# Attention weights times values in two float32r passes, with the values kept as high and low halves side by side

## Chip, core and metric

The program runs on one core of a Trainium2 chip. The metric is the device time of one execution in microseconds; lower is better. Engines are named as in the profile: PE (TensorE), PEld (its weight loads), DVE (VectorE), ACT (ScalarE), POOL (GpSimd), SP (the queue that issues the transfers).

## What is computed

The reference is two blocks of two layers each on 512 tokens of width 1024. The first block has an RWKV layer and a layer of banded attention, each followed by a convolutional feed-forward layer. The second has a layer with two kinds of attention (differential and sparse) and a layer of latent attention. Two places matter here: the banded attention (16 heads of 64, 4 key/value heads, a window of 128) and the sparse one (8 heads of 64 over one shared value head).

```python
def swa_sink_attention(x, k, v, w_q, sinks, w_o):
    ...
    s = jnp.einsum('bnqhgd,bnkhd->bnhgqk', q, kb) * (HEAD_DIM ** -0.5)
    s = jnp.where(mask, s, NEG_INF)
    m = jnp.maximum(jnp.max(s, axis=-1, keepdims=True), sk)
    p = jnp.exp(s - m)
    denom = jnp.sum(p, axis=-1, keepdims=True) + jnp.exp(sk - m)
    o = jnp.einsum('bnhgqk,bnkhd->bnqhgd', p / denom, vb)
    return o.reshape(B, T, ATTN_HEADS * HEAD_DIM) @ w_o

def dsa_attention(...):        # per block of 128 queries, over the selected keys
    ...
    p = jax.nn.softmax(s, axis=-1)
    return jnp.einsum('bhqk,bqkd->bqhd', p, v_sel)
```

## The kernel before

Everything lies feature-major: 1024 features as 8 tiles of 128 partitions by 512 tokens. A dense product keeps its operands as a high and a low part in float32r and runs three passes (`mm3`, L375 to L377); `split` (L322) makes the two parts, the high one with an ACT copy (L325), the low one with a DVE subtraction (L326). Weights arrive by SP, are split the same way (`wload`), and `ahead` loads the next ones early.

**Banded attention** (`swa`, L1365). The work is eight items (`gp`, `blk`): two pairs of key/value heads by four blocks of 128 queries. `scores(it)` makes for each of 8 heads two PE passes (L1407, L1408), a DVE reduction that adds the mask and takes the row's minimum (`submin`, L1502), an ACT exponential (L1410) and a scaling, on POOL for even heads (L1396) and on DVE for odd ones (L1398, after a reciprocal, L1394). `values(it)` turns the probabilities with PE transposes (L1427), copies each 128x512 tile from PSUM with ACT (L1429), multiplies it with 64 columns of the values in plain float32 (L1435: two heads write the two halves of one PSUM tile `po`) and splits `po` into the operand of the output projection (L325, L326). Items are woven: the loop at L1481 runs the values of item i-1 beside the scores of item i (`even` spreads their steps), beside the two late query tiles (`late`) for the first three rounds, and beside the first half of the output projection's first two tiles (`begun`) for the last four. Eight PSUM tiles are shared by all (`ps`, L310). `V` is filled with one ACT copy for each token tile (L1476).

**Sparse attention** (`dsa_parts`, L1744). Four blocks of queries, 3 down to 0. `scores` is as above (L1783, L1784, L1502, L1789), with a bias that POOL adds to the selection (L1776). `values(qb)` turns the probabilities (`turn`, L1807), copies them with ACT (L1811) or, for the last blocks, DVE (L1809), multiplies with `vb` in float32 (L1826), multiplies with gate and denominator `g` on DVE (L1829) and splits (L1830). Values of a block run beside the scores of the next. The projection `w_eo` follows, and its first tiles begin on heads that are done.

The order of the instructions on each engine is fixed when the program is built, by the weaving above and a scheduler that knows the dependences; an engine waits at the head of its queue.

Of the kernel before, what the change touches and what calls it, by code (L numbers as in the profile page):

```python
# [9 lines left out]
F32 = mybir.dt.float32  # L10
F32R = mybir.dt.float32r
AF = mybir.ActivationFunctionType
ALU = mybir.AluOpType
# [4 lines left out]
T = 512  # L18
# [3 lines left out]
TT = 4  # L22
# [216 lines left out]
def run(gen):  # L239
    for _ in gen:  # L240
        pass
# [42 lines left out]
HALF = slice(0, 64), slice(64, 128)  # L284


class Net:
# [1077 lines left out]
    def swa(self):  # L1365
        nc = self.nc
        ident = self.ident
        with self.pool("sw_a") as ap, ExitStack() as es:
            qT = ap.tile([128, 2, KT, T], F32R, name="qT")
            kT = ap.tile([128, 2, 2, T], F32R, name="kT")  # L1370
            kL = ap.tile([128, 2, 2, T], F32R, name="kL")
            V = ap.tile([128, TT, 256], F32, name="V")
            msk = ap.tile([128, 256], F32, name="msk")
            nc.sync.dma_start(out=msk, in_=self.i["c_swa"])
            self.bias_rows()
# [41 lines left out]
            def values(it):  # L1417
                gp, blk = it
                k0 = 0 if blk else 1
                S = SS.pop(it)  # L1420
                PT = {}
                for e in range(2):
                    for kc in range(k0, 2):
                        pt = self.ps()
                        for hg in range(4):
                            o = (kc - k0) * 128
                            nc.tensor.transpose(pt[:, hg * 128 : hg * 128 + 128], S[:, e, hg, o : o + 128], ident)  # L1427
                        PT[e, kc] = op.tile([128, 512], F32, tag="PT", name=self.nm("PT"), bufs=6)
                        nc.scalar.activation(PT[e, kc], pt, AF.Copy)  # L1429
                        yield  # L1430
                po = self.ps()
                for kc in range(k0, 2):
                    for e in range(2):
                        g = 2 * gp + e
                        nc.tensor.matmul(po[64 * e : 64 * e + 64], V[:, blk - 1 + kc, g * 64 : g * 64 + 64], PT[e, kc], start=kc == k0, stop=kc == 1)  # L1435
                    yield
                q = slice(blk * 128, blk * 128 + 128)
                oh, ol = out[gp]
                self.split(oh[:, :, q], ol[:, :, q], po[:].rearrange("p (h q) -> p h q", h=4))
                yield  # L1440

            def query(m, ps, pool):
# [18 lines left out]
            items = [(gp, blk) for gp in range(2) for blk in range(TT)]  # L1461
            with self.pool("sw_p") as pp:
                pss, rr, row = self.first
                row = self.row_sb(row)
                xk = self.hilo(pp, KT, "xk")
                for j in range(KT):
                    self.split(xk[j][0], xk[j][1], self.x[:, j], scale=self.vec("kv_g", j))
                for m in range(2):
                    ps = self.dense_fm(self.i["w_kk"][m], xk, then=self.i["w_kk"][1] if m == 0 else self.i["w_kv"][0][:, :1024])
                    t = pp.tile([128, T], F32, tag="t", name=self.nm("t"), bufs=2)  # L1470
                    nc.vector.tensor_tensor(out=t, in0=ps, in1=row, op=ALU.mult)
                    self.twice(kT[:, :, m], kL[:, :, m], t)
                    for i in range(3 * m, 3 * m + 3):
                        query(i, pss[i], pp)
                even((self.dense_tm(self.i["w_kv"][0], xk, 256,
                                    lambda tt, ps: nc.scalar.activation(V[:, tt], ps[:, :256], AF.Copy, scale=rr[:, tt : tt + 1])), 8), (scores(items[0]), 9))  # L1476
            op = es.enter_context(self.pool("sw_o"))
            out = {0: [op.tile([128, 4, T], F32R, name=f"o{q}0") for q in "hl"]}
            q67 = late()
            begun = chain(*(self.begin(self.i["w_oa"], [(out[0][0][:, j], out[0][1][:, j]) for j in range(4)], m, 4) for m in range(2)))  # L1480
            for i in range(1, 9):  # L1481
                live = [(values(items[i - 1]), 7)]
                if i < 8:
                    live.append((scores(items[i]), 9))
                if i < 4:
                    live.append((take(q67, 6), 6))
                if i == 4:
                    run(q67)
                    out[1] = qT[:, 0, :4], qT[:, 1, :4]
                if i > 4:  # L1490
                    live.append((take(begun, 2), 2))
                even(*live)
# [3 lines left out]
            flat = [qT[:, e, 4:].rearrange("p m t -> p (m t)") for e in range(2)] + [kT[:].rearrange("p e m t -> p (e m t)")]  # L1496
            yg = [t for _ in range(2) for t in self.by_tile(sp.tile([128, 4, T], F32, tag="S", name=self.nm("yg"), bufs=2))]
            self.project(self.i["w_oa"], xs, "ng11", yg, "ng12", 4, "ffn1", [[t[:, f * 1024 : f * 1024 + 1024] for f in range(2)] for t in flat])

    def submin(self, out, ps, mask, mn, first=3e38):  # L1500

# [242 lines left out]
    def dsa_parts(self, ap, qb_, kb, vb, sel, gate):  # L1744

        nc = self.nc
        ident = self.ident
        bts, SS, WD = {}, {}, {}

        head = lambda i: 2 * (i % 4) + i // 4  # L1750

        def load(i):
            bts[head(i)] = self.bias_tile(4 + head(i), ap, f"bias{i}")
# [43 lines left out]
        def values(qb):  # L1797
            q = slice(qb * 128, qb * 128 + 128)
            S, wide = SS.pop(qb), WD.pop(qb)
            PT = {}  # L1800

            def turn(kc):
                PT[kc] = self.wp.tile([128, 2, T], F32, tag="wl", name=self.nm("PT"))
                for e in range(2):
                    pt = self.ps()
                    for j in range(4):
                        nc.tensor.transpose(pt[:, j * 128 : j * 128 + 128], S[:, 4 * e + j, kc * 128 : kc * 128 + 128], ident)  # L1807
                    if qb == 0 or qb < 2 and e:
                        nc.vector.tensor_copy(PT[kc][:, e], pt)  # L1809
                    else:  # L1810
                        nc.scalar.activation(PT[kc][:, e], pt, AF.Copy)  # L1811
                    yield

            yield from turn(0)

            row = self.ps()
            for j in range(4):
                nc.tensor.transpose(row[:, j * 128 : j * 128 + 128], wide[:, j].rearrange("p e d -> p (e d)"), ident)
            g = self.sp.tile([128, 4, 128], F32, tag="sssq", name=self.nm("g"), bufs=2)
            nc.vector.tensor_tensor(out=g, in0=row[:].rearrange("p (h q) -> p h q", h=4), in1=gate[:, 4:, q], op=ALU.mult)  # L1820
            po = self.ps()
            for kc in range(qb + 1):
                if kc < qb:
                    yield from turn(kc + 1)
                for e in range(2):
                    nc.tensor.matmul(po[64 * e : 64 * e + 64], vb[:, kc, 8:72], PT[kc][:, e], start=kc == 0, stop=kc == qb)  # L1826
                yield
            y = self.sp.tile([128, 4, 128], F32, tag="ssacc", name=self.nm("y"), bufs=2)
            nc.vector.tensor_tensor(out=y, in0=po[:].rearrange("p (h q) -> p h q", h=4), in1=g, op=ALU.mult)  # L1829
            self.split(self.oh[:, 4:, q], self.ol[1][:, :, q], y[:])  # L1830
            yield

        return prep(), [((scores(n, qb), 9), (values(qb), 3 * qb + 4), None) for n, qb in enumerate((3, 2, 1, 0))]
# [221 lines left out]
```

## Time and profile before

| | |
|---|---|
| median of 3 runs | 1983.86 us (1981.19 to 1985.35) |
| profiled execution | 1977.79 us, span 1976.0 us |
| granted PE clock, mean | 0.985 |
| PE busy | 1883.4 us, 95% of the span |
| DVE busy | 1337.9 us, 68% |
| ACT busy | 956.5 us, 48% |
| POOL busy | 335.9 us, 17% |
| chain that ended last | PE 76%, DVE 15%, issue 3%, ACT 3%, DMA 2% |
| banded attention, items woven | 899.9 to 971.6 us of the span |
| sparse attention, values | 1619.4 to 1656.8 us |

A busy share is an average over stages with different limits, so the two stretches in the last rows are read by themselves: busy time by engine there, then which engine's instructions follow each other without a hole, then at what spacing they start. Instructions of one engine overlap a little: the start of one to the start of the next is shorter than the time that a row gives for one.

### The profile page before, as it was taken

To read this page: it belongs to the slowest core of one execution; us is meant where nothing else is said; L and a number is where in the kernel's file an instruction comes from. 1 tells how busy PE (TensorE), PEld (TensorE's weight loads), DVE (VectorE), ACT (ScalarE), POOL (GpSimd) and SP (SyncE) were. 2 spreads that over 40 slices of the span, in tenths; PEclk is the share of its full clock that TensorE was granted. 3 is DMA by queue.
4 is the path that set the end of the run, shared out by engine and by line. 5 is a ranking of instruction groups with operands and counts; after the bars stand their busy time and mean duration, and the time that the engine had idled before them with its cause. 6 is when DMAs were issued, how large, how long until landed. Compare 5 with 4: busy or idle time off the path is not lost.

```text
span 1976.0 us, 28014 instructions
## 1 busy us (share of the span) xinstructions
PE 1883.4 (95%) x10610; PEld 1491.1 (75%) x10610; DVE 1337.9 (68%) x2618; ACT 956.5 (48%) x1818; POOL 335.9 (17%) x385
## 2 busy tenths in 40 slices
PE   6999878999999999989999999999999999999998
PEld 4784457788888888966688888889788657787657
DVE  7759888767977742677577777525799566356765
ACT  4546344565644432557655444324443475346662
POOL 3347330432000000133120000000304022010000
PEclk9999988999999999999999999999999989999999
DMA  3230101053332333421123332334422113221102
GB/s 115 91 123 26 44 1 32 20 176 99 107 95 97 97 95 98 133 89 54 42 74 100 106 96 96 90 99 129 156 83 86 48 49 116 89 96 57 40 23 86
DMA packets 55424, 165.53 MB, mean 84 GB/s; under 512 B 6182, under 2 KB 11942, under 8 KB 55290
## 3 DMA queue, kind: packets, MB, share of 16 engines
q1 hardware_dynamic: 55290, 163.76, 26.7%
q8 instruction: 83, 1.36, 0.3%
q14 instruction: 51, 0.42, 0.1%
HBM read 161.61 MB, written 2.13 MB: 83 GB/s over the span
## 4 chain that ended last, share of the span: by engine, by line
PE 76%; DVE 15%; issue 3%; ACT 3%; DMA 2%; POOL 1%; DVEq 0%; POOLq 0%; SPq 0%; ACTq 0%
PE ps L375 19%; PE ps L377 18%; PE ps L376 18%; PE ps L448 5%; DVE wl L326 2%; PE ps L1953 2%; PE ps L1984 1%; DVE x L595 1%; PE ps L1435 1%; PE ps L1971 1%; PE ps L1689 1%; ACT wh L325 1%; DVE xl L329 1%; DVE AB L1159 1%; DVE yg L594 1%
## 5 line engine op out<-in xcount | busy, mean ns | idle before, releaser
L326 DVE TENSOR_TENSOR wl<-wr,wh 128x1024 fp32r<-128x1024 f32 (+2 forms) x279 | 328.0, 1176 | 249.9 <-ACT wh L325 243.1
L325 ACT ACTIVATE wh<-wr 128x1024 fp32r<-128x1024 f32 (+2 forms) x279 | 278.8, 999 | 425.8 <-PE ps L376 288.8
L375 PE MATMUL ps<-xh,wh 128*128 128x512 f32 x856 | 338.8, 396 | 0.0
L377 PE MATMUL ps<-xh,wl 128*128 128x512 f32 x856 | 335.7, 392 | 0.0
L376 PE MATMUL ps<-xl,wh 128*128 128x512 f32 x856 | 332.6, 389 | 0.0
L377 PEld LDWEIGHTS ps<-xh,wl 128*128 128x128 f32 x856 | 160.7, 188 | 37.3
L376 PEld LDWEIGHTS ps<-xl,wh 128*128 128x128 f32 x856 | 160.8, 188 | 35.9 <-issue 1.1
L375 PEld LDWEIGHTS ps<-xh,wh 128*128 128x128 f32 x856 | 160.9, 188 | 33.1 <-issue 1.9
L504 POOL TENSOR_TENSOR rr<-rs,mhalf 128x2 f32<-128x2 f32 (+1 forms) x18 | 19.9, 1108 | 891.8 <-DVE rs L502 874.9
L377 PE MATMUL ps<-hidh,wl 128*128 128x512 f32 (+1 forms) x440 | 152.7, 347 | 1.3 <-DVE wl L326 1.3
L375 PE MATMUL ps<-hidh,wh 128*128 128x512 f32 (+1 forms) x440 | 152.8, 347 | 0.0
L376 PE MATMUL ps<-hidl,wh 128*128 128x512 f32 (+1 forms) x440 | 152.5, 347 | 0.0
L1355 DVE SCALAR_TENSOR_TENSOR cv<-h,vecs,cv 128x510 f32<-128x510 f32 (+1 forms) x176 | 130.5, 747 | 2.9 <-ACT cv L1353 0.6
L448 PE MATMUL ps<-xh,wl 128*128 128x512 f32 (+1 forms) x306 | 104.3, 346 | 5.3 <-DVE wl L326 5.3
L448 PE MATMUL ps<-xh,wh 128*128 128x512 f32 (+1 forms) x306 | 103.4, 347 | 3.0 <-ACT xh L328 3.0
L448 PE MATMUL ps<-xl,wh 128*128 128x512 f32 (+1 forms) x306 | 104.2, 343 | 0.0
L1351 DVE TENSOR_TENSOR h<-ps,row 128x512 f32<-128x512 f32 x88 | 60.1, 686 | 60.3 <-PE ps L377 60.3
L377 PEld LDWEIGHTS ps<-hidh,wl 128*128 128x128 f32 x440 | 83.3, 189 | 12.1 <-DVE wl L326 1.7
L375 PEld LDWEIGHTS ps<-hidh,wh 128*128 128x128 f32 x440 | 83.3, 189 | 10.5
L376 PEld LDWEIGHTS ps<-hidl,wh 128*128 128x128 f32 x440 | 83.3, 189 | 10.2
L1353 ACT ACTIVATE cv<-h,vecs 128x512 f32<-128x512 f32 x88 | 71.3, 812 | 11.7 <-DVE h L1351 11.3
L325 ACT ACTIVATE hidh<-cv 128x512 fp32r<-128x512 f32 x44 | 27.7, 630 | 91.9 <-DVE cv L1359 91.8
(467 smaller groups left out, 4152.5 us busy)
## 6 DMA issues: line engine op xcount, KB each, us to landing
wr<-in_w_up SPq DMA_DIRECT2D x76, 512.0 KB, 3.5
wr<-in_w_down SPq DMA_DIRECT2D x40, 448.0 KB, 3.4
wr<-in_w_down SPq DMA_DIRECT2D x20, 512.0 KB, 3.5
wr<-in_w_e SPq DMA_DIRECT2D x20, 512.0 KB, 3.6
wr<-in_w_or SPq DMA_DIRECT2D x16, 512.0 KB, 3.6
wr<-in_w_upg SPq DMA_DIRECT2D x16, 384.0 KB, 3.0
bias<-brow SPq DMA_DIRECT2D x20, 256.0 KB, 4.2
wr<-in_w_oa SPq DMA_DIRECT2D x9, 512.0 KB, 3.6
```

The lines of the kernel that those rows point to most:

```text
L325: nc.scalar.activation(hi, src, AF.Copy)
L326: nc.vector.tensor_tensor(out=lo, in0=src, in1=hi.bitcast(F32), op=ALU.subtract)
L329: nc.vector.scalar_tensor_tensor(out=lo, in0=src, scalar=scale, in1=hi.bitcast(F32), op0=ALU.mult, op1=ALU.subtract)
L375: mm(out, ah, bh, start=start, stop=False)
L376: mm(out, ah, bl, start=False, stop=False)
L377: mm(out, al, bh, start=False, stop=stop)
L448: self.nc.tensor.matmul(pss[m][:, tok], w[a][:, c], xs[j][b][:, tok], start=j == 0 and i == 0 and tok.start == 0, stop=j == KT - 1 and i == 2,
L504: nc.gpsimd.tensor_tensor(out=rr[:, a:b], in0=rs[:, a:b], in1=self.mhalf[:, a:b], op=ALU.pow)
L1351: nc.vector.tensor_tensor(out=h, in0=ps, in1=row, op=ALU.mult)
L1353: nc.scalar.activation(t, h, AF.Identity, bias=self.vec(f"cb{l}", m), scale=self.vec(f"cw{l}2", m))
L1355: nc.vector.scalar_tensor_tensor(out=t[:, d:], in0=h[:, : T - d], scalar=self.vec(f"cw{l}{2 - d}", m), in1=t[:, d:], op0=ALU.mult, op1=ALU ...
L1953: nc.tensor.matmul(ps[:, :w], qh[:, qb * 128 : qb * 128 + 128], kh[:, :w], start=True, stop=True)
```

## The change

In both attentions the transposed probabilities are kept as a high and a low part (`split`: an ACT copy and a DVE subtraction for each 128x512 tile, instead of one copy). The values too are kept as two float32r parts, side by side as 128 columns. `two_pass` multiplies them: one pass with the high, one with the low part of the probabilities, so that the upper half of the PSUM tile holds the product with the values' high part and the lower half that with the low part. Each head group has a PSUM tile of its own, two for an item instead of one. `joined` adds the halves: for each of the two tiles an ACT copy of one half (64x512) and a DVE addition of the other. In the sparse attention the product with `g` moves from DVE to POOL. The values' parts are made by an ACT copy and a DVE subtraction for each token tile (banded) or by one ACT copy and one POOL subtraction (sparse). The steps of `values` are regrouped (a product is issued one step after its splits), and the shares of the weaving go from 7 to 6 or 4 steps.

```diff
-            V = ap.tile([128, TT, 256], F32, name="V")
+            V = ap.tile([128, TT, 4, 2, 64], F32R, name="V")
...
-                PT = {}
-                for e in range(2):
-                    for kc in range(k0, 2):
+                late = []
+                po = [self.ps() for _ in range(2)]
+                for kc in range(k0, 2):
+                    for e in range(2):
                         pt = self.ps()
                         for hg in range(4):
                             o = (kc - k0) * 128
                             nc.tensor.transpose(pt[:, hg * 128 : hg * 128 + 128], S[:, e, hg, o : o + 128], ident)
-                        PT[e, kc] = op.tile([128, 512], F32, tag="PT", name=self.nm("PT"), bufs=6)
-                        nc.scalar.activation(PT[e, kc], pt, AF.Copy)
+                        ph, pl = (op.tile([128, 512], F32R, tag="P" + n, name=self.nm("P" + n), bufs=3) for n in "hl")
+                        self.split(ph, pl, pt)
+                        late.append((po[e], V[:, blk - 1 + kc, 2 * gp + e], ph, pl, kc == k0, kc == 1))
+                        if len(late) > 1:
+                            self.two_pass(*late.pop(0))
                         yield
-                po = self.ps()
-                for kc in range(k0, 2):
-                    for e in range(2):
-                        g = 2 * gp + e
-                        nc.tensor.matmul(po[64 * e : 64 * e + 64], V[:, blk - 1 + kc, g * 64 : g * 64 + 64], PT[e, kc], start=kc == k0, stop=kc == 1)
-                    yield
+                self.two_pass(*late.pop(0))
+                yield
                 q = slice(blk * 128, blk * 128 + 128)
                 oh, ol = out[gp]
-                self.split(oh[:, :, q], ol[:, :, q], po[:].rearrange("p (h q) -> p h q", h=4))
+                y = self.joined(po)
+                self.split(oh[:, :, q], ol[:, :, q], y[:].rearrange("p (h q) -> p h q", h=4))
                 yield
...
+    def two_pass(self, out, v, ph, pl, start, stop):
+        v = v.rearrange("p a b -> p (a b)")
+        self.nc.tensor.matmul(out, v, ph, start=start, stop=False)
+        self.nc.tensor.matmul(out, v, pl, start=False, stop=stop)
+
+    def joined(self, po):
+        nc = self.nc
+        y = self.sp.tile([128, T], F32, tag="ssacc", name=self.nm("yj"), bufs=2)
+        for e in range(2):
+            own, other = HALF[e], HALF[1 - e]
+            nc.scalar.activation(y[own], po[e][other], AF.Copy)
+            nc.vector.tensor_tensor(out=y[own], in0=po[e][own], in1=y[own], op=ALU.add)
+        return y
+
+    def parts_of_values(self, dst, src, scale):
+        nc = self.nc
+        hi, lo = dst[:, :, 0], dst[:, :, 1]
+        nc.scalar.activation(hi, src, AF.Copy, scale=scale)
+        nc.vector.scalar_tensor_tensor(out=lo, in0=src, scalar=scale, in1=hi.bitcast(F32), op0=ALU.mult, op1=ALU.subtract)
...
+        vp = self.sp.tile([128, TT, 2, 64], F32R, tag="rowsb", name="vp")
+        nc.scalar.activation(vp[:, :, 0], vb[:, :, 8:], AF.Copy)
+        nc.gpsimd.tensor_tensor(out=vp[:, :, 1], in0=vb[:, :, 8:], in1=vp[:, :, 0].bitcast(F32), op=ALU.subtract)
...
-                    if qb == 0 or qb < 2 and e:
-                        nc.vector.tensor_copy(PT[kc][:, e], pt)
-                    else:
-                        nc.scalar.activation(PT[kc][:, e], pt, AF.Copy)
+                    self.split(PT[kc][0][:, e], PT[kc][1][:, e], pt)
...
-                    nc.tensor.matmul(po[64 * e : 64 * e + 64], vb[:, kc, 8:72], PT[kc][:, e], start=kc == 0, stop=kc == qb)
+                    self.two_pass(po[e], vp[:, kc], PT[kc][0][:, e], PT[kc][1][:, e], kc == 0, kc == qb)
...
-            nc.vector.tensor_tensor(out=y, in0=po[:].rearrange("p (h q) -> p h q", h=4), in1=g, op=ALU.mult)
-            self.split(self.oh[:, 4:, q], self.ol[1][:, :, q], y[:])
+            y = self.joined(po)[:].rearrange("p (h q) -> p h q", h=4)
+            nc.gpsimd.tensor_tensor(out=y, in0=y, in1=g, op=ALU.mult)
+            self.split(self.oh[:, 4:, q], self.ol[1][:, :, q], y)
```

What this does to the order is shown at three places. First DVE in the banded attention, where the scores of item (0, 3) are made (S with the higher number) beside the values of item (0, 2). Before:

```order
L1502 ISA S_8160,st_8161<-ps_8164,msk,snk 128x256
L1502 ISA st_8161 128x1
L1398 TENSOR_SCALAR S_8047<-S_8047,st_8048 128x256
L1394 RECIPROCAL st_8161<-st_8161 128x1
L1502 ISA S_8160,st_8161<-ps_8195,msk,snk 128x256
L1502 ISA st_8161 128x1
L1394 RECIPROCAL st_8161<-st_8161 128x1
L1398 TENSOR_SCALAR S_8160<-S_8160,st_8161 128x256
```

Now, at the same place (lines are 25 to 30 further down in the changed file, in `scores` by 1):

```order
L326 TENSOR_TENSOR Pl_8211<-ps_8205,Ph_8210 128x512
L1527 ISA S_8194,st_8195<-ps_8198,msk,snk 128x256
L1527 ISA st_8195 128x1
L1395 RECIPROCAL st_8195<-st_8195 128x1
L326 TENSOR_TENSOR Pl_8229<-ps_8223,Ph_8228 128x512
L1527 ISA S_8194,st_8195<-ps_8237,msk,snk 128x256
L1527 ISA st_8195 128x1
L1395 RECIPROCAL st_8195<-st_8195 128x1
L326 TENSOR_TENSOR Pl_8256<-ps_8250,Ph_8255 128x512
L1399 TENSOR_SCALAR S_8194<-S_8194,st_8195 128x256
```

Between the reductions of the scores now stand the subtractions of the probabilities' low parts, four for such an item; the two additions of `joined` follow further down. The second place is PE, with the products of item (0, 2) before (two heads of one key block each time):

```order
L1435 MATMUL ps_8132<-PT_8061,V 64x512
L1435 MATMUL ps_8132<-PT_8094,V 64x512
L1407 MATMUL ps_8135<-kT,qT 128x256
L1408 MATMUL ps_8135<-kL,qT 128x256
L375 MATMUL ps_8122<-xh_7019,wh_7964 128x512
```

and now, where the pass with a low part stands some rows behind that with the high part:

```order
L1506 MATMUL ps_8072<-Pl_8080,V 128x512
L1505 MATMUL ps_8073<-Ph_8097,V 128x512
L1408 MATMUL ps_8136<-kT,qT 128x256
L1409 MATMUL ps_8136<-kL,qT 128x256
L1408 MATMUL ps_8106<-kT,qT 128x256
L1409 MATMUL ps_8106<-kL,qT 128x256
L1429 MATMUL ps_8143<-ident,S_7945 128x128 x4
L1506 MATMUL ps_8073<-Pl_8098,V 128x512
L1505 MATMUL ps_8072<-Ph_8124,V 128x512
```

Other PE work of the same item fills the place between the two passes. The third place is the end of the sparse attention on DVE, the last block of queries. Before:

```order
L1809 COPY PT_14345<-ps_14362 128x512
L326 TENSOR_TENSOR wl_14409<-wr_14407,wh_14408 128x1024
L1820 TENSOR_TENSOR g_14376<-ps_14371,gate 128x512
L326 TENSOR_TENSOR wl_14444<-wr_14442,wh_14443 128x1024
L1829 TENSOR_TENSOR y_14384<-ps_14378,g_14376 128x512
L326 TENSOR_TENSOR ol_13538<-y_14384,oh_13536 128x4x128
```

and now:

```order
L326 TENSOR_TENSOR PT_14545<-ps_14563,PT_14544 128x512
L326 TENSOR_TENSOR ol_13677<-yj_14533,oh_13675 128x4x128
L1845 TENSOR_TENSOR g_14578<-ps_14573,gate 128x512
L1515 TENSOR_TENSOR yj_14589<-ps_14580,yj_14589 64x512
L1515 TENSOR_TENSOR yj_14589<-ps_14581,yj_14589 64x512
L326 TENSOR_TENSOR wl_14618<-wr_14616,wh_14617 128x1024
L326 TENSOR_TENSOR wl_14653<-wr_14651,wh_14652 128x1024
L326 TENSOR_TENSOR ol_13677<-yj_14589,oh_13675 128x4x128
```

The two weight splits stand now between the additions of `joined` and the last split, where POOL makes the product with `g`.

## Rows read from the trace of the kernel before

**Rows 1.** The page, part 1: busy time, share of the span and instructions of an engine.

```profile
PE 1883.4 (95%) x10610; PEld 1491.1 (75%) x10610; DVE 1337.9 (68%) x2618; ACT 956.5 (48%) x1818; POOL 335.9 (17%) x385
```

**Rows 2.** Busy time by stretch: the stretch, its length, busy us (instructions) of PE, PEld, DVE, ACT and POOL, the granted PE clock, the DMA share and GB/s. The first is the banded attention's woven items, the second the sparse attention's values.

```profile
899.90:971.60 71.70, 69.62 (x358) 43.91 (x356) 51.41 (x212) 53.81 (x157) 22.17 (x42) 1.00 0.10 30
1619.40:1656.80 37.40, 35.64 (x208) 23.48 (x207) 27.62 (x81) 27.55 (x77) 12.89 (x19) 1.00 0.32 96
1604.00:1622.00 18.00, 16.18 (x100) 11.83 (x99) 16.20 (x56) 16.70 (x55) 5.11 (x11) 1.00 0.44 115
1605.00:1612.00 7.00, 6.94 (x41) 4.56 (x41) 6.86 (x26) 6.14 (x21) 0.11 (x1) 1.00 0.00 0
1590.00:1600.00 10.00, 10.00 (x31) 5.43 (x31) 3.98 (x15) 3.85 (x15) 0.00 (x0) 0.55 0.00 0
200.00:250.00 50.00, 44.58 (x279) 23.47 (x278) 44.75 (x96) 18.30 (x43) 16.66 (x28) 1.00 0.13 43
300.00:350.00 50.00, 41.30 (x746) 37.41 (x740) 43.25 (x113) 20.59 (x40) 6.17 (x4) 0.83 0.11 34
```

**Rows 3.** PE in order of time, banded attention: start, duration, line, operation, count. One product of L1435 leaves two records, so "x4" is the products of two heads, which run side by side.

```profile
914.20 0.28 PE L1408 MATMUL ps<-kL,qT 128*128 128x256 f32 x1
914.41 1.08 PE L1435 MATMUL ps<-PT,V 128*64 128x512 f32 x4
915.42 0.39 PE L1407 MATMUL ps<-kT,qT 128*128 128x256 f32 x1
915.64 0.28 PE L1408 MATMUL ps<-kL,qT 128*128 128x256 f32 x1
915.76 0.40 PE L375 MATMUL ps<-xh,wh 128*128 128x512 f32 x1
916.00 0.39 PE L376 MATMUL ps<-xl,wh 128*128 128x512 f32 x1
```

**Rows 4.** The chain that ended last, in order of time: start, us on the chain, what. Two of the 19 groups of L1435 in the banded attention (11 of two records, 7 of four, one of six) and the longest of the 10 groups of L1826.

```profile
936.74 1.86 PE ps L1435 x6
...
966.70 1.54 PE ps L1435 x4
...
1631.40 1.42 PE ps L1826 x4
```

**Rows 5.** DVE in order of time, banded attention, in a piece without a hole.

```profile
945.15 0.69 DVE L326 TENSOR_TENSOR qT<-ps,qT 128x512 fp32r<-128x512 f32 x1
945.76 0.48 DVE L1502 CUSTOM_DVE_ANT_0 S<-ps,msk,snk 128x256 f32<-128x256 f32 x1
...
946.16 0.16 DVE L1394 RECIPROCAL st<-st 128x1 f32<-128x1 f32 x1
946.23 0.47 DVE L1502 CUSTOM_DVE_ANT_0 S<-ps,msk,snk 128x256 f32<-128x256 f32 x1
...
946.62 0.35 DVE L1398 TENSOR_SCALAR S<-S,st 128x256 f32<-128x256 f32 x1
946.89 0.48 DVE L1502 CUSTOM_DVE_ANT_0 S<-ps,msk,snk 128x256 f32<-128x256 f32 x1
```

**Rows 6.** DVE by line, sparse attention from 1619.4 to 1656.8: line, operation, names, shapes, count, busy us, mean ns, idle before.

```profile
L326 DVE TENSOR_TENSOR wl<-wr,wh 128x1024 fp32r<-128x1024 f32 x3 | 3.7, 1221 | 0.0
```

**Rows 7.** DVE in order of time, sparse attention: scores over 384, 256 and 128 keys, the copy of the denominators and the row g, each with the row after it.

```profile
1619.49 0.56 DVE L1502 CUSTOM_DVE_ANT_0 S<-ps,b 128x384 f32<-128x384 f32 x1 [0.16 <-PE ps L1784]
...
1619.97 0.20 DVE L1792 RECIPROCAL st<-st 128x8 f32<-128x8 f32 x1
...
1635.25 0.42 DVE L1502 CUSTOM_DVE_ANT_0 S<-ps,b 128x256 f32<-128x256 f32 x1
...
1635.59 0.42 DVE L1502 CUSTOM_DVE_ANT_0 S<-ps,b 128x256 f32<-128x256 f32 x1
...
1642.80 0.42 DVE L1794 COPY wide<-st 128x512 f32<-128x512 f32 x1
1643.14 0.28 DVE L1502 CUSTOM_DVE_ANT_0 S<-ps,bias 128x128 f32<-128x128 f32 x1
...
1644.85 0.69 DVE L1820 TENSOR_TENSOR g<-ps,gate 128x512 f32<-128x512 f32 x1
1645.45 0.28 DVE L1502 CUSTOM_DVE_ANT_0 S<-ps,bias 128x128 f32<-128x128 f32 x1
1645.66 0.69 DVE L1809 COPY PT<-ps 128x512 f32<-128x512 f32 x1
```

**Rows 8.** DVE and POOL in order of time, in two places. Ahead of the banded items, a DVE instruction on all partitions, then one whose output begins at partition 64 (L336). Then, in the banded stretch, a POOL product of two SBUF tiles and a weight split of two SBUF tiles that DVE begins beside it.

```profile
888.42 0.69 DVE L1444 SCALAR_TENSOR_TENSOR t<-ps,row 128x512 f32<-128x512 f32 x1
889.14 0.69 DVE L336 TENSOR_TENSOR qT<-t,qT 64x512 fp32r<-64x512 f32 x1
...
930.68 1.28 POOL L336 TENSOR_TENSOR qT<-t,qT 64x512 fp32r<-64x512 f32 x1 [0.43 <-ACT qT L335]
930.76 2.28 DVE L326 TENSOR_TENSOR wl<-wr,wh 128x1024 fp32r<-128x1024 f32 x1
```

**Rows 9.** ACT by line in the banded stretch, and POOL by line in the sparse one (columns as in Rows 6).

```profile
L1429 ACT ACTIVATE PT<-ps 128x512 f32<-128x512 f32 x28 | 16.0, 585 | 1.9 <-PE ps L1427 1.8
...
L1776 POOL TENSOR_TENSOR b<-bias,sel 128x384 f32<-128x384 f32 x6 | 5.9, 1005 | 2.0 <-DVE st L1502 2.0
```

More of the change, by code (lines that the diff above doesn't have):

```diff
@@ L1475, in swa @@
                 even((self.dense_tm(self.i["w_kv"][0], xk, 256,
-                                    lambda tt, ps: nc.scalar.activation(V[:, tt], ps[:, :256], AF.Copy, scale=rr[:, tt : tt + 1])), 8), (scores(items[0]), 9))
+                                    lambda tt, ps: self.parts_of_values(V[:, tt], ps[:, :256].rearrange("p (g d) -> p g d", g=4), rr[:, tt : tt + 1])), 8), (scores(items[0]), 9))
             op = es.enter_context(self.pool("sw_o"))
@@ L1481, in swa @@
             for i in range(1, 9):
-                live = [(values(items[i - 1]), 7)]
+                live = [(values(items[i - 1]), 6 if (i - 1) % TT else 4)]
                 if i < 8:
@@ L1802, in turn @@
             def turn(kc):
-                PT[kc] = self.wp.tile([128, 2, T], F32, tag="wl", name=self.nm("PT"))
+                PT[kc] = [self.wp.tile([128, 2, T], F32R, tag=tag, name=self.nm("PT")) for tag in ("wh", "wl")]
                 for e in range(2):
@@ L1820, in values @@
             nc.vector.tensor_tensor(out=g, in0=row[:].rearrange("p (h q) -> p h q", h=4), in1=gate[:, 4:, q], op=ALU.mult)
-            po = self.ps()
+            po = [self.ps() for _ in range(2)]
             for kc in range(qb + 1):
@@ L1825, in values @@
                 for e in range(2):
-                    nc.tensor.matmul(po[64 * e : 64 * e + 64], vb[:, kc, 8:72], PT[kc][:, e], start=kc == 0, stop=kc == qb)
+                    self.two_pass(po[e], vp[:, kc], PT[kc][0][:, e], PT[kc][1][:, e], kc == 0, kc == qb)
                 yield
-            y = self.sp.tile([128, 4, 128], F32, tag="ssacc", name=self.nm("y"), bufs=2)
-            nc.vector.tensor_tensor(out=y, in0=po[:].rearrange("p (h q) -> p h q", h=4), in1=g, op=ALU.mult)
-            self.split(self.oh[:, 4:, q], self.ol[1][:, :, q], y[:])
+            y = self.joined(po)[:].rearrange("p (h q) -> p h q", h=4)
+            nc.gpsimd.tensor_tensor(out=y, in0=y, in1=g, op=ALU.mult)
+            self.split(self.oh[:, 4:, q], self.ol[1][:, :, q], y)
             yield
```

## The prediction

> **What bounds the kernel now.** I read the page's busy times first, then the busy time by stretch, then single engines in order of time. Over the whole span TensorE is busy 95% and DVE 68% [rows 1], which would say that a change that saves TensorE columns wins and that DVE has room. The two stretches that the change touches say something else [rows 2]. In the banded one (71.7 us) PE is busy 69.62 and DVE 51.41 us, in the sparse one (37.4 us) PE 35.64, DVE 27.62. PE is the bound in both, but DVE already stands at 72% and 74%. Durations of neighbours overlap, so everything below is priced from start to start.
>
> **What PE saves.** A plain float32 product of L1435 starts at 914.41 and the next one at 915.42: 1.01 us; one head or two side by side cost the same [rows 3]. Around it 0.09 us more lie before the start (0.21 from the start of L1408 to it, against 0.12 from the L1408 at 915.64 to its successor), and 0.10 in the spacing of the next pair (0.22 against 0.12): 0.19. There are 19 such groups, two of them longer on the chain, 1.86 and 1.54 us [rows 4]: 17 x 1.01 + 1.54 + 1.86 + 19 x 0.19 = 24.2 us. Now 28 products have two passes each of 128 x 512 in float32r; such passes start 0.24 us apart (915.76 to 916.00) [rows 3]: 56 x 0.235 = 13.2. PE saves 11.0 us in the banded stretch. In the sparse one ten groups (9 x 1.01 + 1.42 [rows 4], with ten times 0.19: 12.4) become 40 passes (9.4): 3.0 saved. If PE stayed the bound, this change would give 14 us.
>
> **What DVE gets.** A subtraction or addition over 512 columns with one operand in PSUM takes 0.61 start to start (945.15 to 945.76) [rows 5]. Each of 28 transposed tiles now has one: 28 x 0.605 = 16.9 us. `joined` has two additions for each of eight items: 16 x 0.605 = 9.7, and each pair leaves partition 0 for partition 64 and comes back. An instruction that begins at partition 64 started 0.72 us behind a full one (888.42 to 889.14) [rows 8] where 0.61 is usual [rows 5]; 0.12 for each way is 1.9 more. Together 28.5 us. What DVE did before, priced the same way: 48 score reductions at 0.39 (946.23 to 946.62), eight of half width at 0.26, 56 reciprocals at 0.07 (946.16 to 946.23), 28 scalings at 0.27 (946.62 to 946.89) [rows 5] or 0.20, 12 splits and late query steps at 0.605, four weight splits at 1.14 (1.22 long [rows 6], less an overlap of 0.08): 20.8 + 4.2 + 7.2 + 7.2 + 4.6 = 44.0 (51.41 with overlaps counted twice [rows 2]). After: 72.5 us of dense DVE work, where PE wants 69.6 - 11.0 = 58.6. DVE becomes the bound, and the stretch was 71.7 long.
>
> In the sparse stretch scores cost 8 x 0.48, 8 x 0.34, 8 x 0.21, the gate rows 0.60, the wide copies 0.34 each [rows 7]; weight splits 3 x 1.14 [rows 6], six output splits 0.605, smaller ones 2.4: 8.2 + 2.4 + 1.4 + 3.4 + 3.6 + 2.4 = 21.4 stay. New: 20 low parts, 12.1; eight additions with their changes of partition, 5.8. The four copies at L1809 go to ACT, the four products with `g` to POOL. After: 39.3 us in a stretch that was 37.4 long.
>
> **How dense DVE can be.** DVE waits for PE's transposes, PE for ACT's high parts and DVE's low parts. Where DVE led before, it was busy 16.20 of 18.00 us (0.90), and over its best 7 us 6.86 (0.98) [rows 2]. I take the middle, 0.94: banded 72.5 / 0.94 = 77.1, that is +5.4; sparse 39.3 / 0.94 = 41.8, +4.4. At 0.98 these are +2.3 and +2.7, at 0.90 +8.9 and +6.3.
>
> **The smaller terms.** Ahead of the banded items DVE now makes the low parts of the values, four of 256 columns between four reductions. No row has this form; it lies between a scaling (0.27) and a reduction (0.39) of 256 columns [rows 5], I take 0.36: +1.4, and 0 if PE's products cover it. At the end of the sparse part POOL multiplies with `g`: 1005 ns for 384 columns [rows 9], 1.28 us for 512 [rows 8]. After it come ACT's and DVE's split. PE has the first halves of the projection meanwhile, and DVE two weight splits, 2.3 us. But the trace shows a price: a weight split that DVE began 0.08 us after such a POOL product took 2.28 us [rows 8], not 1.22 [rows 6]; it ended 1.1 us after the product had. So one of the two late weight splits is held: +1.1, 0 if it isn't on the path, and 1.9 if the split behind POOL is waited for too. The Trainium skill ("SBUF — State Buffer", section "Who interferes with whom") says that a Vector instruction with two SBUF inputs and a GpSimd instruction that reads SBUF exclude each other and that whichever is issued later waits; the 2.28 us agree. By that page the eight output splits of the banded part, which now read `yj` from SBUF where they read PSUM, would also wait behind POOL's scalings; by the share of POOL's busy time, 22.17 of 71.70 us [rows 2], that is an estimate of about 0.7 us more; I leave it out of the sum, since no row shows it.
>
> ACT gets 16 copies at 585 ns [rows 9], 9.4 us on 53.81 [rows 2], and in the sparse part 12, 7.0 on 27.55. With 63 of 77 and 35 of 42 us it is covered by DVE; if DVE were not the bound, ACT would be next. The weaving shares only move work. The sum is 5.4 + 4.4 + 1.4 + 1.1 = +12.3 us on the profiled execution's 1977.79, so 1990.1. That execution was 6.1 us under the median of the runs, 1983.86; against the median: 1996 us. The bounds of density give +6 (0.98, the smaller terms on) and +18 (0.90).
>
> **Rivals.** *PE's saving is kept (faster).* DVE closes every hole, and what stands last on it slides under PE's projection: in the banded part the last item (four low parts, join and split, 4.5 us) and two weight splits (2.3), so 72.5 - 6.8 = 65.7, -6.0; in the sparse part the last join and split 2.1 and two weight splits 2.3, 39.3 - 4.4 = 34.9, -2.5; the values' parts are hidden. -8.5 us, 1975.5 against the median. For it: the order puts those weight splits late. Against it: 0.98 was reached for 7 us only [rows 2]. It decides when DVE's holes in both stretches stay under 5 us together.
>
> *DVE is dense, but not more.* At 0.98 with half of that slide (5 us) and 1.4 for the values: 2.3 + 2.7 + 1.4 - 5 = +1.4, 1985.3: no change.
>
> *The clock falls.* PE would be busy 58.6 of 77 us, 76%, with holes. Where PE was busy 41.30 of 50 us before, the granted clock was 0.83, and in a stretch after a quiet one 0.55; but 44.58 of 50 kept 1.00 [rows 2]. At 0.83 (between the two levels of 1.2 and 2.4 GHz) the 92 us of PE work in the two stretches grow by 19; about half lies under DVE's work, so +9 on the forecast: 2005.
>
> **How the numbers follow.** Forecast 0.51, all of it slower; clock 0.14, slower; no change 0.18; saving kept 0.17. A measurement of this kernel tells about 0.2%, 4 us, from no change, so faster 0.17, same 0.19 and slower 0.64 (0.01 of the forecast falls within 4 us). The range goes from 1979 to 2010: +18 and the clock's price above, and below down to the no-change case with the near half of the saving; about 0.10 are left out below and 0.08 above.
>
> **What would show it.** In the changed profile: PE's passes with V 0.235 us apart; the banded stretch about 77 us with DVE's dense work near 72 and PE at 76%; PE waiting for the low parts of the probabilities; the sparse stretch about 42 us; clock 1.00; the weight splits beside POOL's last product near 2.3 us. It is wrong if the banded stretch is under 72 us, or if DVE has holes while PE stands on the chain, or if the loss lies in other stretches.

## The result and the profile after

The changed kernel took 2007.69 us (median of 4 runs, 2005.97 to 2009.38), the kernel before 1982.63 in the same comparison (1981.19 to 1985.35): a ratio of 1.0123, 95% interval 1.0105 to 1.0140. That is some 25 us slower. The forecast was 1996, slower by 12.

The page of the changed kernel's profile, part 1 (it answers [rows 1]):

```profile
PE 1894.3 (94%) x10610; PEld 1512.8 (75%) x10610; DVE 1379.2 (69%) x2686; ACT 975.4 (49%) x1847; POOL 345.0 (17%) x390
```

By this row alone little happened: DVE has 41 us more, PE hardly changed. PE should have 14 us less; it has 11 more, and that is the first hint at a slower clock. The time is found by laying the two traces side by side. The same DVE and ACT instructions start 0.7 us earlier than before up to 860 us, 0.9 us later from 870 us on, just ahead of the banded stretch, and 16.7 us later behind it; ahead of the sparse one they are 18.4 us late, behind it 30.3. So the banded stretch lost **15.8 us**, the sparse one **11.9**, all else 2.6. (This is one execution against one; the medians differ by 25. The table below uses the same reading for every run: the median shift of equal instructions behind a stretch less that ahead of it.)

The step of 1.6 us near 865 has nothing to do with the change. It lies in a projection ahead of the woven items that no edit touches, and there the granted clock (the last but two of the columns of [rows 2]) is lower in this execution. The same work, in the kernel before and in the changed one:

```profile
860.00:872.00 12.00, 11.21 (x50) 8.14 (x51) 3.32 (x5) 2.06 (x3) 2.50 (x5) 1.00 0.34 107
859.30:871.30 12.00, 11.21 (x45) 8.04 (x45) 3.32 (x5) 2.09 (x3) 2.50 (x5) 0.86 0.34 109
```

The same step stands in the traces of e1, e2, e4, e7 and e12 below, not in those of the other runs. Read from 860 us, it would count as a loss of the banded stretch, 17.3 instead of 15.8; the expectations written ahead of the runs (17, 14, 7.9) have it in them.

Busy time by stretch in the changed kernel, columns as in [rows 2]: the banded stretch, the sparse one, and pieces of the banded one:

```profile
901.00:989.50 88.50, 75.32 (x360) 57.50 (x358) 75.78 (x258) 63.49 (x171) 22.59 (x43) 0.87 0.08 25
1638.00:1687.00 49.00, 39.66 (x208) 31.10 (x207) 41.52 (x101) 34.69 (x89) 20.23 (x23) 0.93 0.28 91
901.00:920.00 19.00, 18.06 (x104) 14.62 (x102) 18.02 (x65) 16.93 (x44) 6.99 (x13) 1.00 0.08 29
931.00:941.00 10.00, 8.19 (x35) 6.46 (x35) 8.18 (x28) 6.56 (x18) 3.00 (x6) 0.66 0.01 2
941.00:946.00 5.00, 2.29 (x13) 1.61 (x13) 4.61 (x21) 4.29 (x15) 0.80 (x2) 1.00 0.01 3
946.00:950.00 4.00, 4.00 (x18) 3.52 (x17) 3.44 (x10) 2.18 (x6) 1.91 (x3) 0.57 0.21 40
981.00:989.50 8.50, 7.60 (x23) 5.64 (x23) 4.38 (x6) 3.50 (x6) 0.00 (x0) 0.64 0.22 62
```

Two things stand here. DVE is busy 75.78 of 88.5 us, near the 72.5 of the forecast, but in a stretch 11 us longer than forecast. And the granted clock, 1.00 in the whole stretch before [rows 2], is 0.87: 88.5 x 0.13 = 11.5 us of full-speed TensorE time were not granted, the worst of them behind holes of PE (busy 2.29 of 5 us at 941, then a clock of 0.57). In the sparse stretch it is 49 x 0.07 = 3.4 us. Single passes show the two levels. PE in order of time, first at 2.4 GHz, then at 1.2:

```profile
924.87 0.40 PE L1506 MATMUL ps<-Pl,V 128*128 128x512 f32 x1
925.11 0.28 PE L1408 MATMUL ps<-kT,qT 128*128 128x256 f32 x1
...
935.55 0.79 PE L1505 MATMUL ps<-Ph,V 128*128 128x512 f32 x1 [0.16 <-ACT Ph L325]
936.14 0.63 PE L1506 MATMUL ps<-Pl,V 128*128 128x512 f32 x1
936.57 0.41 PE L1408 MATMUL ps<-kT,qT 128*128 128x256 f32 x1
```

From the pass at 924.87 to the next matmul it is 0.24 us, from that at 936.14 it is 0.43. What made PE wait ahead of that is in the chain that ended last, in order of time (start, us, what):

```profile
927.69 0.23 ACT yj L1514
927.92 0.27 issue
928.19 0.60 ACT S L1411 x2
928.81 0.16 DVE st L1395
928.98 0.38 DVE S L1527
929.36 0.27 DVE S L1399
929.63 0.08 DVE st L1395
929.78 0.62 POOL S L1397
930.45 0.33 PE ps L1429
...
931.92 0.69 DVE yj L1515
932.64 0.69 DVE t L1446
...
933.41 0.60 DVE ol L326
934.00 0.28 DVE S L1399
934.28 0.14 issue
934.41 0.46 PE ps L1429
...
942.32 0.59 DVE yj L1515
943.06 0.25 DVE S L1527
943.62 0.69 DVE yj L1515
944.54 0.48 DVE S L1527
945.09 0.38 PE ps L1408
```

An addition of `joined`, a late query step and an output split stand on DVE ahead of one scaling (L1399, 934.00), for which PE's transposes wait. The last rows are the longest hole of PE in this stretch: a pass of the scores (L1408) waits 2.21 us for a reduction on DVE (L1527), and both additions of one `joined` stand ahead of it. Over the stretch PE waits 13.2 us where it waited 2.1 before; less work of its own to fill such places is the likely reason (how much less, see below), but it is not shown by itself.

### The profile page after: what moved, and what is told of

It is laid out like the page before. It is cut to its first block, busy times and chain, and to the rows that moved or that the text cites. A ratio compares the mean times of both kernels' runs of the same rounds, so it can differ in the third digit from the quotient of the medians.

```text
span 2006.2 us, 28123 instructions
## 1 busy us (share of the span) xinstructions
PE 1894.3 (94%) x10610; PEld 1512.8 (75%) x10610; DVE 1379.2 (69%) x2686; ACT 975.4 (49%) x1847; POOL 345.0 (17%) x390
## 4 chain that ended last, share of the span: by engine, by line
PE 74%; DVE 16%; ACT 4%; issue 3%; DMA 2%; POOL 1%; SPq 0%; POOLq 0%; DVEq 0%; ACTq 0%
PE ps L375 18%; PE ps L377 18%; PE ps L376 18%; PE ps L448 6%; DVE wl L326 2%; PE ps L1978 2%; PE ps L2009 1%; DVE x L595 1%; DMA wr<-in_w_down 1%; PE ps L1996 1%; ACT wh L325 1%; PE ps L1714 1%; DVE AB L1159 1%; DVE xl L329 1%; DVE yg L594 1%
```

## The experiments

All runs in one table: the ratio to the kernel before, and from each trace what the two stretches lost against it (us) and the granted clock from 900 to 1000 us.

| run | ratio (95%) | banded | sparse | clock |
|---|---|---|---|---|
| the change | 1.0123 (1.0105 to 1.0140) | +15.8 | +11.9 | 0.88 |
| e1_banded | 1.0077 (1.0049 to 1.0105) | +15.8 | -0.1 | 0.88 |
| e2_nolow | 1.0030 (1.0012 to 1.0048) | +1.4 | +6.1 | 1.00 |
| e3_nojoin | 1.0017 (1.0000 to 1.0034) | +1.0 | +1.3 | 0.98 |
| e4_fill | 1.0081 (1.0050 to 1.0113) | +12.9 | +6.2 | 0.97 |
| e5_padded | 1.0019 (0.9999 to 1.0038) | -0.5 | -0.1 | 1.00 |
| e6_before_low | 1.0033 (1.0018 to 1.0048) | +5.5 | +0.2 | 1.00 |
| e7_before_fill | 1.0086 (1.0065 to 1.0107) | +6.3 | +7.1 | 0.99 |
| e8_g_on_dve | 1.0122 (1.0098 to 1.0146) | +15.1 | +8.6 | 0.88 |
| e9_half_fill | 1.0095 (1.0071 to 1.0119) | +8.6 | +11.4 | 1.00 |
| e10_late_join | 1.0149 (1.0127 to 1.0171) | +16.8 | +12.4 | 0.88 |
| e11_pool_scalings | 1.0085 (1.0058 to 1.0112) | +8.0 | +11.4 | 0.97 |
| e12_padded_pool | 1.0007 (0.9991 to 1.0023) | +2.8 | +0.2 | 0.98 |

A stretch that no edit touched repeats within 0.2 us where it is that of before (sparse in e1, e5, e6, e12) and within 0.7 where it is the changed one (banded in e1 and e8, sparse in e9, e10 and e11). Three theories were set against each other. D: DVE's amount of work sets the stretches. J: the joins hold the in-order queues of ACT and DVE. C: PE's holes bring the clock down, and that is most of the price.

**e1_banded.** Edit: `dsa_parts` as before, all else changed.

> Only the banded part of the change; the sparse attention is that of the kernel before. The trace of the changed kernel puts 17 us of its loss into the banded stretch and 10 to 11 into the sparse one. If the two are independent this run is 14 to 18 us over the kernel before (1997 to 2001). If one loss is only the echo of the other (the clock, transfers), it is under 8 or over 22.

Measured: +15.8 in the banded stretch, as with the whole change, nothing in the sparse one, 15 us by the runs. The two losses are independent.

**e2_nolow.** Edit, and the same in the sparse part:

```diff
-                        self.split(ph, pl, pt)
+                        nc.scalar.activation(ph, pt, AF.Copy)      # ph and pl are one tile
```

> The changed kernel without the subtractions that make the low parts of the probabilities (28 banded, 20 sparse); the second pass reads the high part again, so PE, ACT and the joins are as in the changed kernel. Theory D (DVE's work sets both stretches): 16.9 and 12.1 us of DVE work go, DVE has about as much room as before, and PE's saving of 14 us shows: 8 to 14 us under the kernel before. Theory J (the joins hold ACT's and DVE's queues, and PE waits behind them): the joins are still there; the loss shrinks by less than half, 12 to 20 us over before.

Measured: 0.3% over before; the banded loss is 1.4, the sparse one 6.1, the clock back at 1.00. Between the two: most of the loss goes, against J, but with 16.9 us of DVE work gone and PE's saving kept there is still no gain, against D.

**e3_nojoin.** Edit:

```diff
-                y = self.joined(po)
+                y = po[0]
```

> The changed kernel without the joins: the output split reads one of the two PSUM tiles directly (so one half of the values' product is left out), and in the sparse part DVE multiplies with g, as before. Both passes and the low parts stay. Theory J: the loss goes nearly whole, within 4 us of the kernel before or up to 8 under it, and PE's waits behind the join copies go with it. Theory D: DVE loses 11.6 us of work banded and 3.4 sparse, about half of what the low parts are; 10 to 16 us over before stay.

Measured: 0.17% over, banded +1.0, sparse +1.3, clock 0.98. J's number. But e2 and e3 together forbid adding up: 16.9 us of DVE work taken away gave back 14.4, the joins (11.6 of DVE, 9.4 of ACT) gave back 14.8, of a loss of 15.8. Taking away either one nearly suffices, so the two do not add up. Without the joins three things go at once: the copies on ACT, the additions on DVE, and the time for which the second PSUM tile of an item is held. No run separates them.

**e4_fill.** Edit, and the same in the sparse part:

```diff
-                        for hg in range(4):
+                        for hg in (0, 1, 2, 3, 0, 1, 2, 3):
```

> The changed kernel with every transpose of the probabilities made twice into the same place: useless PE work of 28 x 0.44 = 12.3 us in the banded stretch and 20 x 0.44 = 8.8 in the sparse one, nothing else. Theory C (most of the loss is the granted clock, which fell to 0.83 to 0.91 in the banded stretch because PE waits): the clock there comes back to 0.97 or more and the time is the same as the changed kernel's or up to 8 us lower. Theory D or J without the clock: the transposes stand in the chain from the probabilities to the product, so the time rises by 8 to 20 us.

Measured: 0.8% over before where the change was at 1.23%: 21 us of useless PE work and some 8 to 9 us **faster** (1998.72 against 2007.69 us; by the ratios 0.42%, with intervals that overlap a little; by the stretches 2.9 and 5.7 us less). The banded clock is 0.97, the sparse one 1.00. As C had it. In the sparse part it isn't the clock alone. The last POOL product takes 1.30 us here instead of the 2.30 shown under e8, so a collision with a weight split is gone too:

```profile
1677.98 1.30 POOL L1854 TENSOR_TENSOR yj<-yj,g 128x512 f32<-128x512 f32 x1 [5.83 <-DVE yj L1515]
```

**e7_before_fill.** The same edit in the kernel before.

> The kernel before with the transposes of the probabilities made twice in both attentions, as in the run with the changed kernel. Where PE is the bound, all of 12.3 + 8.8 us shows: 17 to 23 us slower. If less than 12 shows, PE had room before too, and the comparison with the changed kernel's filled run says nothing on the clock.

Measured: +6.3 and +7.1 by the stretches, 17 us by the runs, at the lower end of what was expected. The same work that costs 17 us where PE is the bound gives 8 to 9 back in the changed kernel. For the banded stretch this makes an account: filled and changed, 12.9; less the fill's price, 6.3; leaves 6.6 for the change at a clock near 1.00. The changed kernel's 15.8 less 6.6 is 9.2 for the clock, where 11.5 was not granted. The account takes it that the fill costs as much in the changed kernel, where it can fall into PE's waits; if it costs less there, the change costs more and the clock less. In the sparse part the same account gives 6.2 - 7.1 = -0.9, which no other run bears out.

**e9_half_fill.** Edit: the transposes twice for `e == 0` only, banded part only.

> The changed kernel with the transposes of the probabilities made twice for one of the two heads' groups in the banded part only: half of the useless PE work of the full fill there, 6.2 us; the sparse part as changed. Theory C as it stands now: the banded stretch loses 6 to 7 us at full clock, and 10 to 11 more by the granted clock; a fill costs what it costs in the kernel before (7.9 us of trace for 12.3 of PE, so about 4 here) and gives back clock. If half the fill brings the clock back as the whole one did, the stretch is 10 to 12 us over before, less than the changed kernel's 17 and the filled one's 14. If the clock is not what matters, it lies at 17 plus 4 or more.

Measured: +8.6 in the stretch, under the expected 10 to 12, with the clock at 1.00 all along; the untouched sparse part repeats (+11.4). Its busy time, columns as above:

```profile
904.50:986.50 82.00, 71.87 (x419) 57.15 (x418) 76.03 (x259) 64.15 (x172) 22.93 (x43) 1.00 0.09 27
```

DVE's 76.03 us are those of the changed kernel (75.78), PE still waits 10.1 us, but at the full clock, and 7.2 us are gone. The longest hole is still there, and the clock stays at 1.00 behind it, so a hole of this size does not by itself bring it down:

```profile
947.36 0.39 PE L1408 MATMUL ps<-kT,qT 128*128 128x256 f32 x1 [2.06 <-DVE st L1527]
```

As the useless work can't have made the stretch shorter by itself, the change costs at most 8.6 us at the full clock, and at least 7.2 of its 15.8 are the clock, with one reserve: a fill also changes the order in the other queues (laid against the changed kernel's order, some 50 of DVE's 258 instructions and 50 of ACT's 171 stand elsewhere), and what that gave was not separated.

**e5_padded.** Edit: each head's values in 128 columns of which 64 are zeros, three passes, both heads into one tile; the sparse part as before.

```diff
-        self.nc.tensor.matmul(out, v, ph, start=start, stop=False)
-        self.nc.tensor.matmul(out, v, pl, start=False, stop=stop)
+        self.nc.tensor.matmul(out, vh, ph, start=start, stop=False)
+        self.nc.tensor.matmul(out, vl, ph, start=False, stop=False)
+        self.nc.tensor.matmul(out, vh, pl, start=False, stop=stop)
```

> Banded part alone (the sparse attention is that of the kernel before), with the low parts of the probabilities and float32r passes kept, but without joins: each head's values lie in 128 columns of which 64 are zeros, both heads add into one PSUM tile in three passes (high x high, high x low, low x high), and the output is split from it as before. PE has 28 more passes than in the changed kernel (6.6 us), 4.5 us fewer than before. If the joins (their hand-offs and 11.6 us of DVE, 9.4 of ACT) are what tips the stretch over, the banded stretch is within 4 us of that before and the clock in it at 0.97 or more. If the low parts alone suffice to slow it, it stays 8 us or more over.

Measured: the stretch is 0.5 us shorter than before, the clock 1.00, the ratio 1.0019 with 1 just inside its interval. Its busy time:

```profile
903.00:975.00 72.00, 69.20 (x388) 54.95 (x387) 65.66 (x243) 54.07 (x159) 21.41 (x43) 1.00 0.09 30
```

With the low parts kept, 28 passes more than the change and no joins, PE is at 96% again. This run alters two things at once, though: the 28 passes are 6.6 us of PE work, as much as the half fill of e9, which by itself gave back 7.2 us. That the loss goes with the joins alone is shown by e3.

**e6_before_low.** Edit in the kernel before: a subtraction into an unread tile behind each copy (L1429).

> The kernel before, with one DVE subtraction more for each of the 28 transposed tiles of the banded part, written to a place that nobody reads: 16.9 us of DVE work, PE unchanged. If DVE's work by itself set the changed stretch, this is 6 us or more slower than the kernel before. If PE still sets it, because nobody waits for these subtractions, it is within 3 us.

Measured: +5.5 in the stretch, 0.33% by the runs, between the two expectations. The 16.9 us of DVE work cost a third of themselves although nobody waits for the results; they stand ahead of instructions that are waited for, which is the likely reason. The clock stays at 1.00. So DVE's work costs time without any fall of the clock. That 5.5 is also the forecast's +5.4 means nothing: that was for 28.5 us of DVE work and with PE's saving.

**e11_pool_scalings.** Edit:

```diff
-                    if i % 2 == 0:
+                    if i % 4 != 3:
                         nc.gpsimd.tensor_tensor(...)
```

> The changed kernel with half of DVE's scalings in the banded part (14 of 28) on POOL: 3.7 us of DVE work less, 9 of POOL more. If the stretch goes with DVE's work and the clock with PE's holes, the loss of 17 falls by 4 to 9, more than the work that was taken away. If POOL's longer scaling (0.61 against 0.27) in the chain to the transposes counts more, the loss is the same or grows.

Measured: banded +8.0. 3.7 us of DVE work less give back 7.8, with the clock at 0.97: more than the work, as expected of C.

**e10_late_join.** Edit: one `yield` more ahead of `joined`, shares 7 and 5.

> The changed kernel with the joins of the banded part one step of the weaving later, the same work in another order, so that the copy of a PSUM half no longer stands at the head of ACT's queue while PE still makes the last pass. If this wait at the head of the queue (9.0 us of ACT in the trace) starts PE's holes, the banded loss falls from 17 to under 10 us with the clock at 0.95 or more. If the amount of work does, it stays within 3 us of the changed kernel's.

Measured: +16.8, clock 0.88, no better by the runs. But the edit did not take away the wait that it was aimed at. The waits of ACT for the last pass in this stretch (us, times, longest), in the changed kernel and in this run:

```profile
ACT yj L1514 <- PE ps L1506: 9.0, 10, 2.2
ACT yj L1515 <- PE ps L1507: 7.9, 9, 2.0
```

So the run shows that one step later does not help; whether this wait at the head of ACT's queue starts PE's holes stays open, and J in this form is not tested.

**e8_g_on_dve.** Edit: `nc.vector` for `nc.gpsimd` in the product with `g`.

> The changed kernel with the product with g back on DVE (4 x 0.6 us) instead of POOL. If the hand-off to POOL and the exclusion of POOL's product and DVE's weight splits (2.30 and 3.44 us in the trace where 1.28 and 2.4 are usual) cost what the trace suggests, the sparse part loses 3 to 6 us less than the changed kernel's 11 to 12. If DVE's amount of work is what counts there, it loses 2 us more.

Measured: the sparse loss is 8.6, 3.3 less, as expected of the hand-off; by whole runs the 3 us are not to be told (1.0122). Some 1 us of it may be clock (0.96 in this stretch against 0.94). What the rest consists of shows at the end of the sparse part of the changed kernel, in order of time (DVE, POOL, ACT, PE):

```profile
1679.82 3.44 DVE L326 TENSOR_TENSOR wl<-wr,wh 128x1024 fp32r<-128x1024 f32 x2
1679.86 2.30 POOL L1854 TENSOR_TENSOR yj<-yj,g 128x512 f32<-128x512 f32 x1 [3.69 <-DVE yj L1515]
...
1682.20 0.63 ACT L325 ACTIVATE oh<-yj 128x512 fp32r<-128x512 f32 x1 [2.16 <-POOL yj L1854]
...
1682.88 0.78 PE L375 MATMUL ps<-oh,wh 128*128 128x512 f32 x2 [1.29 <-ACT oh L325]
```

POOL begins 0.04 us behind the first weight split and takes 2.30 us instead of the 1.29 to 1.51 of the other three; the second weight split waits for POOL, so the two take 3.44 instead of 2.4; and PE waits 1.29 us for the part that ACT makes afterwards. In e8 the same place reads, on DVE:

```profile
1680.20 1.23 DVE L326 TENSOR_TENSOR wl<-wr,wh 128x1024 fp32r<-128x1024 f32 x1
1681.35 0.68 DVE L1854 TENSOR_TENSOR yj<-yj,g 128x512 f32<-128x512 f32 x1
1681.95 1.22 DVE L326 TENSOR_TENSOR wl<-wr,wh 128x1024 fp32r<-128x1024 f32 x1
```

**e12_padded_pool.** The edits of e5 and e11 together.

> The banded part with padded values in three passes and no joins, the sparse part of the kernel before, and in addition half of DVE's scalings on POOL. The version without this was even with the kernel before. If DVE still set its stretch, this one is 1 to 4 us under the kernel before; if PE does, it is the same within 2 us; if POOL's scalings are late, it is 1 to 4 us over.

Measured: 1.0007, no difference by the runs; the stretch is 2.8 us longer than before, as expected if POOL's longer scalings come late. No version here beats the kernel before by more than its interval.

## Why the prediction was right, and where not

**Right: the sign, and that DVE's work is its reason.** DVE's new work in the two stretches outweighs PE's saving: the loss goes without the low parts (e2) or without the joins (e3), and 6.6 (e4 less e7) to 8.6 us (e9) of it stand in the banded stretch at the full clock too. The time, 2007.7, lies in the range, but the sum gave only half of the loss, 12 of 25 us; the range reached so far up because it had the price of a rival, the clock, in it. DVE's prices held: the low parts take 0.59 to 0.61 us start to start (682 ns busy), the additions 0.59 or 0.73, the values' parts 0.39 each (0.36 taken).

**Not borne out: PE's saving of 11 us.** A pass behind another does start 0.235 us after it. But in e2, whose PE work is that of the changed kernel, PE is busy 64.64 us at the full clock:

```profile
900.40:975.20 74.80, 64.64 (x363) 50.84 (x362) 63.86 (x231) 63.94 (x173) 24.26 (x43) 1.00 0.10 29
```

That is 5.0 us less than the 69.62 before, where the forecast took 11.0 off. In e5, with PE at 96%, the same prices give 4.5 us less (84 passes, 19.7 us, against 24.2); it was busy 69.20, hardly less than before, and its passes stand 0.27 us apart on average. Part of e2's 64.64 is the end of a matmul that nothing covers ahead of a hole, so how much of the 11 is real stays open.

Busy and idle time of DVE by line, banded stretch of the changed kernel, columns as in [rows 6]:

```profile
L1527 DVE CUSTOM_DVE_ANT_0 S<-ps,msk,snk 128x256 f32<-128x256 f32 x48 | 22.8, 476 | 2.9 <-PE ps L1409 2.4
L326 DVE TENSOR_TENSOR Pl<-ps,Ph 128x512 fp32r<-128x512 f32 x28 | 19.0, 682 | 2.3 <-ACT Ph L325 2.2
L1515 DVE TENSOR_TENSOR yj<-ps,yj 64x512 f32<-64x512 f32 x16 | 11.0, 685 | 2.4 <-ACT yj L1514 2.2
```

DVE's holes are spread evenly: it waits for PE, for ACT's high parts and for ACT's join copies, 12.7 us in all, while PE's lines are about 60% of the chain in this stretch. No engine is the bound; PE, DVE and ACT hand over to one another in a ring. The forecast had named this as a sign of being wrong (DVE has holes while PE stands on the chain), and as to DVE being the bound it was. PE waits little for the low parts, which the forecast also named (0.5 us); it waits for ACT's high parts and DVE's reductions (3.3 us each) and for the scalings.

**Mis-sized: DVE's work, and the clock taken at 1.00.** The forecast put 72.5 us of dense work at a density of 0.94 into 77.1 us, +5.4. DVE was busy 75.78 us of 88.5, 0.86. At the full clock, in e9, it was busy 76.03 of 82.0: 0.93, the density of the forecast. So the density held for the clock that was assumed; the work was 3.3 us short, and 75.8 / 0.94 = 80.6 would have been +8.9, where e9 measured +8.6. The rest, 7 to 9 us, is the clock. The work came out short because DVE's 51.41 us before were put down to "overlaps counted twice" and 44.0 taken instead. A stretch's busy time counts no overlap twice (the groups of its lines add up to 63.8 us); part of the difference is instructions that were held, such as the four weight splits, 5.9 us instead of 4.6. (The +6 that goes with a density of 0.98 is +7.5 by its own terms, 2.3 + 2.7 + 1.4 + 1.1.)

**Mis-sized: the rival's chance.** "The clock falls" had the right mechanism, holes of PE at 76% busy, and a price of +9 on the forecast (2005, measured 2007.7), but a chance of 0.14. It was given so little because one stretch kept 1.00 with PE busy 44.58 of 50 us [rows 2]. The forecast's own stretch, 58.6 of 77, was nearer to the other row that it quoted, 41.30 of 50 at 0.83. Read by the nearest row, as the unknown prices were, the rival deserved far more. It was not certain either: in e9 PE is busy 71.87 of 82 us and in e2 64.64 of 74.8, with holes, and both kept 1.00.

**Wrong: DVE's bound as a sum.** The forecast took DVE's work as what sets the time, so that each us of it counts about once. The loss of 15.8 us shrank by 7.8 when 3.7 us of DVE work went to POOL (e11), by 14.8 without the joins' 11.6 (e3), by 14.4 without the low parts' 16.9 (e2): the first few us count twice, since they also give clock back, and behind them there is little left to gain.

**The sparse part.** Forecast +4.4 +1.1, measured +11.9. 3.4 are clock not granted. The product on POOL was priced at 1.1, e8 shows 3.3 for all four: both directions of the exclusion occurred, POOL behind a weight split and a weight split behind POOL, and the split behind it was waited for. The remaining 5 to 6 (some 1 us of e8's 3.3 may be clock) are near the 4.4 of DVE's work, but they were not taken apart further, and e4 less e7 does not find them.

**The values' parts.** They were put at +1.4, 0 if PE's products cover them. The same instructions are 0.9 us late at 870 to 890 us and 0.6 late right ahead of the items, so the three parts that stand there cost nothing.

**Left out rightly:** the output splits of the banded part, now with two operands in SBUF, were not held by POOL's scalings where the trace of the stretch has them: 682 ns for four with `ol`, 686 for three with `qT`, as before.

## What to carry to other kernels

When work is taken from a busy TensorE and given to an engine that it waits for, reckon the time at a lower clock too: look for the stretch of the same trace whose holes on PE are nearest to those that the change will make, and give its granted clock a real chance in the forecast. It is a case to price, no rule: stretches with much the same holes ran at 1.00 and at 0.87 here. Saved PE time is only a gain if PE has other work ready at that place; a change that makes holes there can cost twice, and useless matmuls in the holes are a quick test of it (look at the order of the other queues as well, which they shift). Before two traces are laid side by side, see that the clock is the same just ahead of the stretch; a step there is easily taken for a loss of the stretch. Two engines that read SBUF side by side (a POOL product, a DVE instruction with two SBUF operands) should not be put next to each other at the end of a stage.

## What was not expected of the hardware

Useless matmuls made the kernel faster: half a fill of 6.2 us of PE work took 7.2 us off the stretch, and a full fill 8 to 9 us off the program.

The clock also falls at places that the change does not touch, and not in every execution. One is that near 865 us, shown with the result. Another lies ahead of the sparse stretch, in the changed kernel:

```profile
1610.00:1620.00 10.00, 10.00 (x35) 5.67 (x33) 4.65 (x16) 4.55 (x16) 0.00 (x0) 0.57 0.00 0
```

and in e4_fill:

```profile
1610.00:1620.00 10.00, 9.70 (x52) 5.88 (x52) 8.42 (x31) 8.32 (x31) 0.24 (x1) 1.00 0.00 0
```

Before it was 0.55 at this place of the program [rows 2]. In e2, e3, e4 and e11 the instructions between the two stretches catch up 4 to 5 us, as much as a good part of the spread between runs of one kernel. So a few us of difference between two single executions are no verdict on a change; a difference of stretches is.
